# Gate and up projections by seven products: four of a pair's products summed in one PSUM bank and two in another, and taken in another order

## The chip, the cores and the metric

The kernel runs on one core of one Trainium2 chip. The metric is the device time of one execution in microseconds (us). A core has a TensorE (PE) that multiplies matrices, a VectorE (DVE), a ScalarE (ACT) and a GpSimd (POOL) for element-wise work, and DMA queues. TensorE writes its results to eight accumulation banks (PSUM), from which DVE and ACT read.

## The reference, cut to what matters

One decoder layer over 1056 tokens (1024 of a prompt, 32 of eight samples), all in float32: a mixing sub-layer, then a SwiGLU feed-forward, then a gated per-layer input. The change is in the feed-forward:

```python
f = _rms(x, n_ffn_pre)
f = (jax.nn.silu(f @ w_gate) * (f @ w_up)) @ w_down      # 1024 -> 2816 -> 1024
x = x + _rms(f, n_ffn_post)
x = x + jax.nn.sigmoid(x @ w_ple_gate) * (p @ w_ple)
```

## The kernel before, in words

The tokens stand in three groups of 352 (groups 0, 1, 2). Each float32 operand is split into a high and a low part (`split`, L162 to L165: an ACT cast makes the high part, a DVE subtraction the low part), and a product of a weight block and an operand is three matmuls of 128x352 per block of 128 rows: high by high, high by low, low by high.

The feed-forward has 22 columns of 128 hidden channels, two to a *slab*. A column (the code calls one call of `gate_up` a slot: slot 0 and slot 1 of a slab) has a gate weight `wg` and an up weight `wu`. For token group 2 a column is done directly: 24 matmuls for the gate, 24 for the up. Groups 0 and 1 together are done by a seven-product scheme (a 2x2 block product with seven multiplications instead of eight): seven products of 12 matmuls each. Two use a half of `wg` by itself (with the operands `B11` and `B21`), one a half of `wu` (operand `T4`), and four use sums of both weights (`S1` with `T1`, `S2` with `T2`, `S3` with `T3`, `S4` with `B22`). GpSimd makes the four sums, in place in the raw weights (`w_sums`, L980), after `wg` and `wu` have been split; then they are split themselves into two tiles, one with S2 and S4, one with S1 and S3 (in the trace, tiles `sh` and `sl`).

The list `WALK` sets the order: steps 0 to 4 do slabs 0 to 4 for group 2 alone, steps 5 to 10 do slabs 5 to 10 for all three groups (below: three-group steps), steps 11 to 15 do slabs 0 to 4 for groups 0 and 1 (below: two-group steps). Slot 0 of each step has, after its first products, the down projections of the step before (`pending`): 24 or 16 products of six matmuls.

What sets the order: TensorE's matmuls are pinned in program order (`mm`, L126). The other engines' instructions are put in order by a scheduler at build time and then run strictly in that order. Split weights live in a ring of eight buffers, tag `wp` (`w_tile`; a high and a low tile each, so four weights at a time), raw weights in a ring of three, tag `wr`. Weights are made in the order of the list `ITEMS`, up to four items ahead of the one in use (`need`). A new tile takes the buffer that comes free first in the program, and its writer waits until TensorE has read the old tile there for the last time. PSUM tiles (`bank`) come from a ring of eight in the same way.

In `gate_up` before the change, every product takes a bank of its own, and the sums of products are made on DVE: `p1` (first product, copied by ACT at L1019), then adds of a product each (`add`, L1014).

Of the kernel before, what the change touches and what calls it, by code (L numbers as in the profile page):

```python
# [13 lines left out]
ALU = mybir.AluOpType  # L14
# [47 lines left out]
def trunk_kernel(  # L62
# [61 lines left out]
    def mm(*args, **kw):  # L124

        ins = te.matmul(*args, **kw)  # L126
        if pinned[0]:
            tc.keep_in_program_order(ins)

    def bank():  # L130
        return psum.tile([P, 512], F32, tag="b", name=nm("b"))

    def tmp(n, s="t", dt=F32):
        return spool.tile([P, n], dt, tag="tmp", bufs=6, name=nm(s), padded_shape=[P, NX])
# [138 lines left out]
                    w_load(js[0])  # L273
        return made[k]

    def gemm(ps, ops, start=True, stop=True):

        last = len(ops) - 1
        for i, (wh, wl, xh, xl) in enumerate(ops):
            mm(ps, wh, xh, start=start and i == 0, stop=False)  # L280
            mm(ps, wh, xl, start=False, stop=False)
            mm(ps, wl, xh, start=False, stop=stop and i == last)

    def ops8(w, xs):

# [703 lines left out]
    def ops4(w, x):  # L989

        return [(w[0][:, k, :], w[1][:, k, :], x[0][:, k, :], x[1][:, k, :]) for k in range(4)]

    def quarter(w, h):
        return tuple(t[:, 4 * h : 4 * h + 4, :] for t in w)

    def gate_up(items, slot, gs, pending):

        ig, iu, is_ = items
        n = N

# [12 lines left out]
        def add(out, a, ps):  # L1013
            ve.tensor_tensor(out, a, ps, op=ALU.add)  # L1014

        wg = need(ig)
        if 0 in gs:
            p1 = tmp(n, "p1")
            se.copy(p1, product(quarter(wg, 0), f7["B11"]))  # L1019
        if 2 in gs:  # L1020
            sl = tmp(n, "sl")
            se.activation(sl, direct(wg), AF.Silu)
        if 0 in gs:
            c11 = tmp(n, "c11")
            add(c11, p1, product(quarter(wg, 1), f7["B21"]))
# [4 lines left out]
        if 2 in gs:  # L1030
            ve.tensor_tensor(sl, sl, direct(wu), op=ALU.mult)
        for g in gs:
            if slot == 0:
                new_hid[g] = half(g, F32R, "hid")
        if 2 in gs:
            hid_put(2, slot, sl)
        if pending and 0 not in gs:
            pending()
        if 0 not in gs:
            return  # L1040
# [7 lines left out]
        if 2 in gs:  # L1048
# [8 lines left out]
        se.activation(p1, p1, AF.Silu)  # L1057
        ve.tensor_tensor(u3, u3, p1, op=ALU.mult)
        hid_put(1, slot, u3)

    os_ = [None] * G

# [203 lines left out]
```

## Time and profile before

| | |
|---|---|
| time, median of 3 runs | 1122.58 us (1121.98 to 1122.92) |
| the profiled execution's own time | 1121.84 us |
| its span, first to last instruction | 1120.1 us |
| TensorE busy | 1108.9 us (99%) |
| DVE, ACT, POOL busy | 748.4, 440.7, 179.5 us |

The span is what the rows below are laid out on: times in them are us from its start. An engine's busy time counts its instructions; the time in which it waits stands as idle time before an instruction, with what ended it. Steps 5 to 10 run from about 388 to 790 us, steps 11 to 15 from there to about 980 us.

### The profile page before, as it was taken

How to read it: one execution, taken by the hardware profiler on the slowest of the kernel's cores; microseconds unless marked ns; L12 is line 12 of the kernel's file. 1: busy time of each engine (PE TensorE's matmuls, PEld its weight loads, DVE VectorE, ACT ScalarE, POOL GpSimd, SP SyncE). 2: the span in 40 equal slices, each digit the busy share in tenths (PEclk: the TensorE clock that was granted, in tenths of full speed). 3: DMA queues.
4: the chain of work that ended last, by engine and by line, in shares of the span. 5: the costliest groups of instructions: out<-in, count | busy, mean ns of one | idle time of the engine just before them, and what ended most of it. 6: DMA issues, size and time to landing. Idle time of an engine off the chain costs nothing.

```text
span 1120.1 us, 17702 instructions
## 1 busy us (share of the span) xinstructions
PE 1108.9 (99%) x7171; PEld 1090.8 (97%) x7171; DVE 748.4 (67%) x1244; ACT 440.7 (39%) x782; POOL 179.5 (16%) x152
## 2 busy tenths in 40 slices
PE   8999999999999999999999999999999999999998
PEld 8999988899999999999999999999999999999998
DVE  6667468985879955355554555557887877789532
ACT  8323276664646524331321314124424334366220
POOL 0045132200000041011111101111132123100000
PEclk9999999999999999999999999999999999999999
DMA  8121311272543312111110212112212222246211
GB/s 288 57 70 43 119 41 38 83 265 71 206 159 132 114 38 76 39 61 54 38 57 20 75 38 76 39 39 93 104 57 77 74 76 79 96 161 215 91 58 39
DMA packets 35265, 99.54 MB, mean 89 GB/s; under 512 B 4180, under 2 KB 14708, under 8 KB 35184
## 3 DMA queue, kind: packets, MB, share of 16 engines
q1 hardware_dynamic: 33856, 96.65, 25.6%
q10 hardware_dynamic: 1328, 1.77, 0.5%
q8 instruction: 56, 0.92, 0.4%
q14 instruction: 25, 0.20, 0.1%
HBM read 88.30 MB, written 10.11 MB: 88 GB/s over the span
## 4 chain that ended last, share of the span: by engine, by line
PE 88%; DVE 6%; ACT 3%; DMA 1%; issue 1%; POOL 0%; SPq 0%; DVEq 0%; ACTq 0%; POOLq 0%
PE b L126 88%; ACT a L634 1%; DVE wl L165 1%; DMA xr<-in_x_dram 1%; DVE mx L626 1%; DVE a L671 1%; ACT wh L164 1%; POOL wr L980 0%; DVE h L366 0%; PE b L120 0%; DMA c<-in_gains_dram 0%; DVE o L1107 0%; DVE x L1111 0%; DVE a L734 0%; DVE p L1014 0%
## 5 line engine op out<-in xcount | busy, mean ns | idle before, releaser
L126 PE MATMUL b<-fh,wh 128*128 128x352 f32 x808 | 260.7, 323 | 0.0
L126 PE MATMUL b<-fh,wl 128*128 128x352 f32 x808 | 259.3, 321 | 0.0
L126 PE MATMUL b<-fl,wh 128*128 128x352 f32 x808 | 259.0, 321 | 0.0
L126 PE MATMUL b<-hid,wh 128*128 128x352 f32 x1056 | 252.5, 322 | 1.7 <-DVE o L1107 1.2
L164 ACT CAST wh<-wr 128x1024 fp32r<-128x1024 f32 (+1 forms) x139 | 142.9, 1030 | 249.6 <-PE b L126 206.6
L165 DVE TENSOR_TENSOR wl<-wr,wh 128x1024 fp32r<-128x1024 f32 (+1 forms) x139 | 171.7, 1238 | 63.8 <-ACT wh L164 63.6
L126 PEld LDWEIGHTS b<-hid,wh 128*128 128x128 f32 x1056 | 182.3, 188 | 2.5 <-issue 1.5
L126 PE MATMUL b<-hid,wl 128*128 128x352 f32 x528 | 169.0, 320 | 0.0
L980 POOL TENSOR_TENSOR wr<-wr 128x512 f32<-128x512 f32 x44 | 63.4, 1441 | 622.3 <-DVE wl L165 451.8
L126 PEld LDWEIGHTS b<-fl,wh 128*128 128x128 f32 x808 | 151.8, 188 | 0.0
L126 PEld LDWEIGHTS b<-fh,wl 128*128 128x128 f32 x808 | 151.8, 188 | 0.0
L126 PEld LDWEIGHTS b<-fh,wh 128*128 128x128 f32 x808 | 151.6, 188 | 0.0
L1077 DVE TENSOR_TENSOR o<-o,b 128x352 f32<-128x352 f32 x240 | 114.7, 514 | 27.3 <-PE b L126 27.2
L126 PE MATMUL b<-fh,sh 128*128 128x352 f32 x352 | 113.6, 323 | 0.0
L126 PE MATMUL b<-fl,sh 128*128 128x352 f32 x352 | 112.8, 320 | 0.0
L126 PE MATMUL b<-fh,sl 128*128 128x352 f32 x352 | 112.7, 320 | 0.0
L126 PE MATMUL b<-h,wh 128*128 128x352 f32 x480 | 106.1, 327 | 1.3 <-ACT h L364 0.9
L165 DVE TENSOR_TENSOR sl<-wr,sh 128x1024 fp32r<-128x1024 f32 x44 | 53.7, 1222 | 75.5 <-ACT sh L164 75.5
L126 PEld LDWEIGHTS b<-hid,wl 128*128 128x128 f32 x528 | 99.0, 187 | 0.0
L164 ACT CAST sh<-wr 128x1024 fp32r<-128x1024 f32 x44 | 45.7, 1047 | 130.9 <-POOL wr L980 91.3
L126 PEld LDWEIGHTS b<-h,wh 128*128 128x128 f32 x480 | 82.6, 190 | 2.6 <-DVE h L366 1.3
L126 PE MATMUL b<-h,wl 128*128 128x352 f32 x240 | 66.3, 325 | 0.0
(150 smaller groups left out, 1593.3 us busy)
## 6 DMA issues: line engine op xcount, KB each, us to landing
wr<-in_w_gu_dram SPq DMA_DIRECT2D x64, 512.0 KB, 3.3
wr<-in_w_dn_dram SPq DMA_DIRECT2D x32, 512.0 KB, 3.5
wr<-in_w_pg_dram SPq DMA_DIRECT2D x14, 512.0 KB, 3.7
x<-in_x_dram SPq DMA_DIRECT2D x6, 704.0 KB, 7.7
x1d<-x SPq DMA_DIRECT2D x6, 704.0 KB, 3.5
x<-x1d SPq DMA_DIRECT2D x6, 704.0 KB, 6.2
out_y_dram<-yo SPq DMA_DIRECT2D x24, 176.0 KB, 1.8
wr<-in_w_out_b_dram SPq DMA_DIRECT2D x8, 512.0 KB, 3.3
```

What stands on the lines that cost most here:

```text
L126: ins = te.matmul(*args, **kw)
L164: fix(se.copy(hi, src))
L165: fix(ve.tensor_tensor(lo, src, hi.bitcast(F32), op=ALU.subtract))
L626: ve.tensor_reduce(mx, t, axis=AX.X, op=ALU.max)
L634: se.activation(t[:, c, :], t[:, c, :], AF.Exp, bias=nmx[:, c : c + 1], scale=scale, accum_out=sm[:, c : c + 1])
L671: ve.copy_predicated(tk, m4(0).bitcast(mybir.dt.int32), v4(cur[kv]))
L980: ge.tensor_tensor(out, a, b, op=op)
L1077: ve.tensor_tensor(o, o, v, op=ALU.add)
```

## The change

Products of one pair are no longer all in banks of their own. A bank `row` takes the first gate product (operand `B11`), is copied out as `p1`, and stays: later products are added onto it by TensorE (no start flag), and it is read again between them. A bank `col` takes the product S1 and, after that has been copied out, S4 on top. In a three-group step `row` takes four products (B11, S2, S3, T4) and is read after each; in a two-group step it takes three, and T4 has its own bank. DVE adds go from seven of a product each to three (three groups) or four (two groups); ACT gets two or three more copies of a bank (L1023 of the changed kernel). The order of the products changes: in a three-group step from gate, direct gate, gate, direct up, S2, S3, T4, S1, S4 to gate, direct gate, gate, S1, S2, S4, S3, direct up, T4; in a two-group step from gate, gate, T4, S2, S3, S1, S4 to gate, gate, S1, S2, T4, S3, S4.

```diff
-    def gemm(ps, ops, start=True, stop=True):
+    def gemm(ps, ops, start=True, stop=True, onto=False):
...
-            mm(ps, wh, xh, start=start and i == 0, stop=False)
...
+            mm(ps, wh, xh, start=start and i == 0, stop=False, skip_group_check=onto)
...
-        def product(w, x):
-            ps = bank()
-            gemm(ps[:, :n], ops4(w, x))
+        def product(w, x, ps=None, start=True):
+            onto = ps is not None
+            ps = ps if onto else bank()
+            gemm(ps[:, :n], ops4(w, x), start, onto=onto)
             turn(12)
             return ps[:, :n]
...
-        def add(out, a, ps):
+        def add(a, ps, s):
+            out = tmp(n, s)
             ve.tensor_tensor(out, a, ps, op=ALU.add)
+            return out
+
+        def copied(ps, s):
+            out = tmp(n, s)
+            se.copy(out, ps)
+            return out
...
         if 0 in gs:
-            p1 = tmp(n, "p1")
-            se.copy(p1, product(quarter(wg, 0), f7["B11"]))
+            row = bank()
+            p1 = copied(product(quarter(wg, 0), f7["B11"], row), "p1")
...
-        if 2 not in gs:
+        s = need(is_)
+        col = bank()
+        p5 = copied(product(s["S1"], f7["T1"], col), "p5")
+        u2 = copied(product(s["S2"], f7["T2"], row, False), "u2")
+
+        def c12():
+            t = add(u2, product(s["S4"], f7["B22"], col, False), "c12")
+            se.activation(t, t, AF.Silu)
+            return t
+
+        if third:
+            g1 = c12()
+            u1 = add(p5, product(s["S3"], f7["T3"], row, False), "u1")
+            ve.tensor_tensor(u1, u1, g1, op=ALU.mult)
+            hid_put(1, slot, u1)
+            third_up()
+            ve.tensor_tensor(c11, c11, product(quarter(wu, 1), f7["T4"], row, False), op=ALU.mult)
+            hid_put(0, slot, c11)
+        else:
             p4 = product(quarter(wu, 1), f7["T4"])
-        s = need(is_)
-        add(p1, p1, product(s["S2"], f7["T2"]))
-        u3 = tmp(n, "u3")
-        add(u3, p1, product(s["S3"], f7["T3"]))
-        c21 = tmp(n, "c21")
-        if 2 in gs:
-            p4 = product(quarter(wu, 1), f7["T4"])
-        add(c21, u3, p4)
-        ve.tensor_tensor(c21, c21, c11, op=ALU.mult)
-        hid_put(0, slot, c21)
-        p5 = product(s["S1"], f7["T1"])
-        add(u3, u3, p5)
-        add(p1, p1, p5)
-        add(p1, p1, product(s["S4"], f7["B22"]))
-        se.activation(p1, p1, AF.Silu)
-        ve.tensor_tensor(u3, u3, p1, op=ALU.mult)
-        hid_put(1, slot, u3)
+            ps = product(s["S3"], f7["T3"], row, False)
+            u3 = copied(ps, "u3")
+            u1 = add(p5, ps, "u1")
+            ve.tensor_tensor(u3, u3, p4, op=ALU.add)
+            ve.tensor_tensor(u3, u3, c11, op=ALU.mult)
+            hid_put(0, slot, u3)
+            g1 = c12()
+            ve.tensor_tensor(u1, u1, g1, op=ALU.mult)
+            hid_put(1, slot, u1)
```

**TensorE, step 14 (two groups), from slot 0's T4 on.** One row for the first of a product's 12 matmuls. The operands are `fh_4142` T4, `fh_4137` T2, `fh_4097` T3, `fh_3829` T1, `fh_4037` B22, `fh_3708` B11, `fh_3906` B21. Before:

```order
L126 MATMUL b_9115<-fh_4142,wh_8839 128x352
...
L126 MATMUL b_9134<-fh_4137,sh_8916 128x352
...
L126 MATMUL b_9149<-fh_4097,sh_8920 128x352
...
L126 MATMUL b_9168<-fh_3829,sh_8920 128x352
...
L126 MATMUL b_9183<-fh_4037,sh_8916 128x352
...
L126 MATMUL b_9208<-fh_3708,wh_8961 128x352
...
L126 MATMUL b_9223<-fh_3906,wh_8961 128x352
...
L126 MATMUL b_9242<-fh_4142,wh_9029 128x352
...
L126 MATMUL b_9261<-fh_4137,sh_9103 128x352
```

After:

```order
L126 MATMUL b_9102<-fh_4142,wh_8778 128x352
...
L126 MATMUL b_8878<-fh_4097,sh_8872 128x352
...
L126 MATMUL b_9073<-fh_4037,sh_8868 128x352
...
L126 MATMUL b_9159<-fh_3708,wh_8913 128x352
...
L126 MATMUL b_9174<-fh_3906,wh_8913 128x352
...
L126 MATMUL b_9200<-fh_3829,sh_9059 128x352
...
L126 MATMUL b_9159<-fh_4137,sh_9055 128x352
```

From the end of slot 0's T4 to slot 1's first product with a sum there were seven products, and there are four. That first product used the tile of S2 and S4 (`sh_9103`); now it uses the tile of S1 and S3 (`sh_9059`).

**ACT, the same place.** Here `wh_8981` is the high part of slot 1's `wu`, `sh_9055` and `sh_9059` are those of the sums (S2 with S4, S1 with S3), `wr_` are raw weights. After:

```order
L1023 COPY u_9100<-b_8878 128x352
L164 CAST wh_8981<-wr_8876 128x1024
L1023 COPY u_9127<-b_8878 128x352
L164 CAST hid_9065<-u_9127 128x352
L164 CAST sh_9055<-wr_8782 128x1024
L1060 ACTIVATE c_9147<-c_9147 128x352
L164 CAST sh_9059<-wr_8876 128x1024
```

In the built program the cast of `wh_8981` waits for the last high-part matmul of slot 0's T4, whose weight `wh_8778` stood in its buffer. Before, the cast of `wh_9029` (slot 1's `wu`) waited for slot 0's T4 too (weight `wh_8839`). In the three-group steps the buffer for slot 1's `wu` is now that of slot 0's S2 and S4, so that its cast waits for S4. The cast of S1 and S3 is still behind that of S2 and S4, now with a Silu (L1060) between.

**DVE, step 12, slot 0.** `hid_` is the low part of group 1's hidden block of the slot before, `sl_` the low part of S2 and S4, `c_` the gate sum. Before:

```order
L1107 TENSOR_TENSOR o_3284<-o_3284,b_8017 128x1408
L1058 TENSOR_TENSOR u_8024<-u_8024,p_7950 128x352
L1111 SCALAR_TENSOR_TENSOR x_7871<-o_3284,c_72,x_7871 128x352 x2
L165 TENSOR_TENSOR hid_7829<-u_8024,hid_7829 128x352
L1014 TENSOR_TENSOR c_8106<-p_8091,b_8107 128x352
L165 TENSOR_TENSOR sl_8082<-wr_7704,sh_8081 128x1024
```

After:

```order
L1129 TENSOR_TENSOR o_3284<-o_3284,b_7970 128x1408
L165 TENSOR_TENSOR hid_7780<-u_8003,hid_7780 128x352
L1133 SCALAR_TENSOR_TENSOR x_7824<-o_3284,c_72,x_7824 128x352 x2
L1080 TENSOR_TENSOR u_8005<-u_8005,c_8023 128x352
L165 TENSOR_TENSOR sl_8034<-wr_7656,sh_8033 128x1024
L165 TENSOR_TENSOR hid_7781<-u_8005,hid_7781 128x352
L1018 TENSOR_TENSOR c_8073<-p_8056,b_8058 128x352
```

The hidden block's low part and the gate sum stood ahead of `sl_` and now stand behind it.

More of the change, by code (lines that the diff above doesn't have):

```diff
@@ L274, in need @@
         return made[k]
-    def gemm(ps, ops, start=True, stop=True):
+    def gemm(ps, ops, start=True, stop=True, onto=False):
         last = len(ops) - 1
         for i, (wh, wl, xh, xl) in enumerate(ops):
-            mm(ps, wh, xh, start=start and i == 0, stop=False)
-            mm(ps, wh, xl, start=False, stop=False)
-            mm(ps, wl, xh, start=False, stop=stop and i == last)
+            mm(ps, wh, xh, start=start and i == 0, stop=False, skip_group_check=onto)
+            mm(ps, wh, xl, start=False, stop=False, skip_group_check=onto)
+            mm(ps, wl, xh, start=False, stop=stop and i == last, skip_group_check=onto)
     def ops8(w, xs):
@@ L1011, in direct @@
             return ps[:, :n]
-        def add(out, a, ps):
+        def add(a, ps, s):
+            out = tmp(n, s)
             ve.tensor_tensor(out, a, ps, op=ALU.add)
+            return out
[3 more added lines that the diff above has]
+            return out
+        third = 2 in gs
         wg = need(ig)
         if 0 in gs:
-            p1 = tmp(n, "p1")
-            se.copy(p1, product(quarter(wg, 0), f7["B11"]))
-        if 2 in gs:
+            row = bank()
+            p1 = copied(product(quarter(wg, 0), f7["B11"], row), "p1")
+        if third:
             sl = tmp(n, "sl")
@@ L1023, in gate_up @@
         if 0 in gs:
-            c11 = tmp(n, "c11")
-            add(c11, p1, product(quarter(wg, 1), f7["B21"]))
+            c11 = add(p1, product(quarter(wg, 1), f7["B21"]), "c11")
             se.activation(c11, c11, AF.Silu)
@@ L1029, in gate_up @@
         wu = need(iu)
-        if 2 in gs:
-            ve.tensor_tensor(sl, sl, direct(wu), op=ALU.mult)
         for g in gs:
```

10 lines of the change are left out of this document (6 added, 4 removed).

## The prediction, made before the changed kernel was timed

> **What bounds the kernel now.** I read the page first: its first line, the busy times and the chain that ended last.
>
> ```profile
> span 1120.1 us, 17702 instructions
> PE 1108.9 (99%) x7171; PEld 1090.8 (97%) x7171; DVE 748.4 (67%) x1244; ACT 440.7 (39%) x782; POOL 179.5 (16%) x152
> PE 88%; DVE 6%; ACT 3%; DMA 1%; issue 1%; POOL 0%; SPq 0%; DVEq 0%; ACTq 0%; POOLq 0%
> ```
>
> TensorE works 99% of the span, and the chain lies on it. Next the table by stage, over the feed-forward, with TensorE's waits in its last part (windows, then waits from 800 to 1000 us):
>
> ```profile
> core 0: us, PE busy (x) PEld busy (x) DVE busy (x) ACT busy (x) POOL busy (x), PEclk, DMA share, GB/s
> 400.00:800.00 400.00, 400.00 (x2523) 400.00 (x2522) 226.76 (x376) 115.99 (x178) 69.59 (x52) 1.00 0.17 55
> 800.00:900.00 100.00, 98.29 (x615) 97.57 (x614) 83.17 (x126) 38.27 (x53) 22.37 (x16) 1.00 0.25 80
> 900.00:1000.00 100.00, 100.00 (x635) 100.00 (x634) 75.47 (x125) 40.87 (x59) 22.14 (x16) 1.00 0.28 90
> PE b L126 <- DVE o L1107: 1.2, 1, 1.2
> PE b L126 <- DVE hid L165: 0.5, 1, 0.5
> ```
>
> From 400 to 800 us TensorE has no gap at all; from 800 to 1000 it loses 1.7 us, at two waits for DVE. So relieving DVE can win 2 us at most, and the changed kernel issues the same matmuls. The question is only whether the new order makes TensorE wait.
>
> **The change: what it removes and adds.** The rows for the two kinds of work (groups by line, DVE and ACT):
>
> ```profile
> L1014 DVE TENSOR_TENSOR p<-p,b 128x352 f32<-128x352 f32 x66 | 34.0, 515 | 6.1 <-PE b L126 5.5
> L1019 ACT COPY p<-b 128x352 f32<-128x352 f32 x22 | 9.7, 442 | 0.9 <-PE b L126 0.9
> ```
>
> DVE loses four adds in each of the 12 three-group pairs and three in each of the 10 two-group pairs: 78 x 0.515 = 40 us. ACT gains two and three copies: 54 x 0.442 = 24 us. Both lie under a TensorE that is 100% busy, with DVE at 57% from 400 to 800 us and ACT at 29%: I cost them at nothing. Were the cover gone, they would be worth what TensorE waits for these engines, the 1.7 us above.
>
> **The wait that it moves: the split sums.** In slot 1 of a two-group step the sums S1 to S4 can be made only after slot 1's `wu` has been split, and its cast waits for the buffer that slot 0's T4 product reads. Step 14 shows the whole chain (timeline, four engines; `wh` is the cast of `wu`, `sh` the casts of the sums, `sl` their low parts):
>
> ```profile
> 918.96 0.32 PE L126 MATMUL b<-fh,wl 128*128 128x352 f32 x1
> 919.12 0.32 PE L126 MATMUL b<-fh,sh 128*128 128x352 f32 x1
> 932.46 0.32 PE L126 MATMUL b<-fh,sh 128*128 128x352 f32 x1
> 919.20 1.05 ACT L164 CAST wh<-wr 128x1024 fp32r<-128x1024 f32 x1 [0.85 <-PE b L126]
> 920.28 1.23 DVE L165 TENSOR_TENSOR wl<-wr,wh 128x1024 fp32r<-128x1024 f32 x1 [0.68 <-ACT wh L164]
> 921.64 1.29 POOL L980 TENSOR_TENSOR wr<-wr 128x512 f32<-128x512 f32 x1 [13.56 <-DVE wl L165]
> 923.02 2.90 POOL L980 TENSOR_TENSOR wr<-wr,wr 128x512 f32<-128x512 f32 x2
> 926.00 1.45 POOL L980 TENSOR_TENSOR wr<-wr 128x512 f32<-128x512 f32 x1
> 927.48 2.00 ACT L164 CAST sh<-wr 128x1024 fp32r<-128x1024 f32 x2 [2.20 <-POOL wr L980]
> 928.57 1.23 DVE L165 TENSOR_TENSOR sl<-wr,sh 128x1024 fp32r<-128x1024 f32 x1 [1.83 <-ACT sh L164]
> 930.14 1.22 DVE L165 TENSOR_TENSOR sl<-wr,sh 128x1024 fp32r<-128x1024 f32 x1
> 930.26 0.50 ACT L1057 ACTIVATE p<-p 128x352 f32<-128x352 f32 x1 [0.78 <-DVE p L1014]
> ```
>
> Slot 0's T4 is done at 919.12 (call it 0). The sums leave POOL at 927.45 (8.33), their casts end at 929.48 (10.36), their low parts at 929.80 and 931.36 (10.68 and 12.24). TensorE meanwhile does seven products, 13.34 us or 1.906 each, and takes up S2, whose tile came first, at 932.46: 2.7 us in hand, without a gap.
>
> Now only four products lie between (S3, S4, and slot 1's B11 and B21): 4 x 1.906 = 7.62 us. And the first sum wanted is S1, whose tile comes second. Its first two matmuls need the cast alone, the third (0.32 us on) the low part: 7.94. I put the chain together in the changed queues. Up to POOL's end, 8.33, it is unchanged. ACT casts S2 and S4 to 9.4, then the Silu (0.50) that now stands between, then S1 and S3 to about 10.9. DVE makes the first low part to 10.7, then a multiplication (about 0.5) that waits for this Silu, to 11.1, then the second low part (1.22), to 12.3. TensorE goes on at 12.35 instead of 7.94: **4.4 us lost in slot 1 of each two-group step, 5 x 4.4 = 22.0 us**. Queued behind the waiting matmul on TensorE is everything else, so the loss is paid in full. In step 11 part of it falls earlier: there the copy of S2 out of `row` stands behind the cast of `wu` on ACT, so S3 waits some 2 us, and S1 that much less. Bounds: 3.9 if the Silu costs nothing, 4.9 if POOL is as slow as in step 12 and the rest slips with it; 19.5 to 24.5 us.
>
> Slot 0 of these steps has 16 down products before its sums and is not late. In the three-group steps the chain of slot 1 takes (timeline of one, from slot 0's T4 on):
>
> ```profile
> 606.58 0.32 PE L126 MATMUL b<-fh,sh 128*128 128x352 f32 x1
> 618.51 0.52 DVE L165 TENSOR_TENSOR hid<-u,hid 128x352 fp32r<-128x352 f32 x1
> ```
>
> 12.0 us to the end of the last `sl`, just ahead of the second row. Now it starts at the end of slot 0's S4, and S1 comes after S3, T4, B11, B21 and two direct products as long as two each: 8 x 1.906 = 15.2 us. In the changed queues the cast of S1 and S3 stands behind a cast of `hid`, which waits for DVE, which is held at the first low part until about 10.7; that adds 2 us, to some 14.1. It is in time by 1.4 us: nothing, with 6 x 1 us as the upper end.
>
> **The reads between products.** TensorE must not add to a bank before it has been read. S4 follows the copy of S1 with one product between, 1.906 us; a copy is 0.44 and starts about 0.2 after the product. 1.2 us are left, enough for one cast of 1.05 ahead of it on ACT. In the built order none stands there but in step 11 (counted above). I take nothing.
>
> **DVE in step 12, slot 0.** The second wait above, in rows:
>
> ```profile
> 819.97 0.33 PE L126 MATMUL b<-hid,wh 128*128 128x352 f32 x1
> 820.80 0.43 PE L126 MATMUL b<-hid,wh 128*128 128x352 f32 x1 [0.51 <-DVE hid L165]
> 819.13 1.61 DVE L165 TENSOR_TENSOR hid<-u,hid 128x352 fp32r<-128x352 f32 x1
> 821.47 1.22 DVE L165 TENSOR_TENSOR sl<-wr,sh 128x1024 fp32r<-128x1024 f32 x1 [0.30 <-ACT sh L164]
> ```
>
> The down product at 819.97 waits for `hid`, 0.67 us beyond its cadence. In the changed order `hid` stands behind `sl`, which ends at 822.69, so `hid` comes at about 823.2, where it came at 820.74: **+2.5 us** (0 to +3.5). The other wait, 1.2 us for the bank that L1107 reads, in step 13, should shrink, since DVE has fewer adds ahead: **-1.2** (-2.0 to 0; `row` now holds one of the eight banks there, against it).
>
> **The clock.** What a gap of 4 us does to it, from windows at the start, in the middle and at the end:
>
> ```profile
> 4.95:8.37 3.42, 2.15 (x8) 1.25 (x8) 2.70 (x6) 2.92 (x6) 0.00 (x0) 1.00 1.02 341
> 8.37:11.79 3.42, 3.42 (x13) 3.42 (x13) 2.36 (x5) 2.10 (x5) 0.00 (x0) 0.50 1.02 357
> 865.11:868.52 3.41, 2.20 (x15) 1.94 (x13) 2.91 (x3) 1.52 (x2) 0.00 (x0) 1.00 0.16 41
> 868.52:871.93 3.41, 3.41 (x22) 3.41 (x23) 3.41 (x8) 0.00 (x0) 0.00 (x0) 1.00 0.29 113
> 1114.29:1117.70 3.41, 1.36 (x9) 1.07 (x7) 1.04 (x2) 0.46 (x1) 0.00 (x0) 1.00 0.00 0
> 1117.70:1120.10 2.40, 0.00 (x0) 0.00 (x0) 0.00 (x0) 0.00 (x0) 0.00 (x0) 0.50 0.20 75
> ```
>
> The granted clock changes at multiples of 3.41 us. After a stretch with 8 matmuls, and after one with 1.36 us busy, it was 0.50 in the next; after one with 15 it stayed 1.00. A gap of 4.4 us leaves one stretch with at least 2.2 us idle, wherever it falls, so I expect a half-clock stretch behind each. A full one does 13 matmuls instead of 22: 9 x 0.159 = 1.4 us; partly under the gap, 1.3. Four gaps of slot 1 and that of step 12 make **5 x 1.3 = 6.5 us** (0 to 10, the latter with two stretches for some).
>
> The Trainium skill has a rule on this, "TensorE: Matmul & The Clock Gate", section "HAM oscillation — how this bites in real kernels": in short, no idle gaps over about 3.4 us. By the table in the same page's "What's actually happening" the clock drops after a whole idle window; here S1's first two matmuls break the gap, and it would stay. The last rows above speak against so strict a reading.
>
> **Sum.** 22.0 + 2.5 - 1.2 + 6.5 = 29.8 us on 1121.84, the profiled execution's own time (its span and 1.7 us around it): 1151.6. The median of the runs is 0.7 above that execution: **1152 us**.
>
> **Rivals.**
> - *The clock stays at 1.00*, if two matmuls in the gap or a partly busy stretch are enough. For it: the stretch with 15 matmuls. Against it: the one with 1.36 us busy. 1121.84 + 22.0 + 2.5 - 1.2 + 0.7 = 1146.
> - *The three-group steps wait too*: their margin of 1.4 us is eaten by ACT, where the `hid` cast ahead of the sums waits for a DVE that is itself late. Six slots of 1 us, and clock with some: 1152 + 9 = 1161. Against it: ACT is 29% busy there.
> - *Not slower: the sums are in time and DVE's relief is what remains.* Slot 1's chain would have to be shorter than 7.94 us. For it: 78 fewer instructions ahead on DVE, and the two waits of 1.7 us gone give 1121. Against it: cast, low part and POOL alone end at 8.33, and none of these waited for DVE's adds in the rows above.
>
> **How the numbers follow.** The forecast 0.68, clock stays 0.16, three-group waits 0.08, not slower 0.08. The likeliest's own range is 1146 to 1159. With the low ends (19.5 + 0 - 2.0 + 0 = 17.5 on 1122.5) and the high ones (24.5 + 3.5 + 10 = 38) it is 1140 to 1161, which takes in the second case and most of the third. A measurement of this kernel can tell about 0.2% from no change. Of the last case half would be over 0.2% faster, half within it: faster 0.04, same 0.04, slower 0.92.
>
> **What would show it.** Between about 790 and 1000 us TensorE's row should lose some 25 us in five gaps, each before the third matmul of an S1 product (`b<-fh,sl`), ended by DVE's `sl`; one of 3 us before a `hid` matmul in step 12; and clock of 0.50 after them. From 400 to 800 us it should have no gap. DVE's busy time should fall by 40 us and ACT's rise by 24. No gap before S1, or one ended by something else than the sums, would prove the chain wrong; a gap of the right size with the clock at 1.00, the second case.

## The result

The changed kernel takes **1162.49 us** (median of 5 runs, 1161.75 to 1166.45) where the kernel before takes 1122.29 us (median of 5 runs, 1121.98 to 1122.92) beside it: a ratio of 1.0365 with a 95% interval of 1.0353 to 1.0376, **40 us slower**. The forecast was 1152 us with a range of 1140 to 1161. The direction, the place and the main mechanism were right. The size was 10 us short, and the measured time lies above the range: the terms for `hid` and for the clock were too small.

### The profile page after: what moved, and what is told of

The parts are those of the page before. It is cut to its first block, busy times and chain, and to the rows that moved or that the text cites. A ratio compares the mean times of both kernels' runs of the same rounds, so it can differ in the third digit from the quotient of the medians.

```text
span 1160.3 us, 17669 instructions
## 1 busy us (share of the span) xinstructions
PE 1124.6 (97%) x7171; PEld 1100.8 (95%) x7171; DVE 722.0 (62%) x1166; ACT 465.1 (40%) x836; POOL 180.9 (16%) x152
## 4 chain that ended last, share of the span: by engine, by line
PE 78%; DVE 7%; ACT 5%; POOL 4%; DMA 3%; issue 1%; SPq 0%; POOLq 0%; ACTq 0%; DVEq 0%
PE b L126 78%; POOL wr L981 4%; DVE wl L165 2%; DMA wr<-in_w_gu_dram 1%; ACT wh L164 1%; DVE sl L165 1%; ACT a L635 1%; DMA xr<-in_x_dram 1%; ACT sh L164 1%; DVE mx L627 1%; DMA a<-in_dmask_dram 1%; DMA x<-x1d 1%; DVE a L672 1%; SPq L341 0%; DVE h L367 0%
## 5 line engine op out<-in xcount | busy, mean ns | idle before, releaser
L126 PE MATMUL b<-hid,wh 128*128 128x352 f32 x1056 | 255.2, 324 | 6.5 <-DVE hid L165 3.7
L126 PE MATMUL b<-fh,sh 128*128 128x352 f32 x352 | 117.8, 335 | 14.0 <-ACT sh L164 12.3
L126 PE MATMUL b<-fh,sl 128*128 128x352 f32 x352 | 117.3, 333 | 5.0 <-DVE sl L165 5.0
L126 PE MATMUL b<-fl,sh 128*128 128x352 f32 x352 | 116.3, 330 | 0.0
L126 PEld LDWEIGHTS b<-fh,sh 128*128 128x128 f32 x352 | 69.1, 196 | 15.7 <-ACT sh L164 13.7
```

## The profile after

First the page of the changed kernel (its first line, the busy times, the shares of the chain that ended last):

```profile
span 1160.3 us, 17669 instructions
PE 1124.6 (97%) x7171; PEld 1100.8 (95%) x7171; DVE 722.0 (62%) x1166; ACT 465.1 (40%) x836; POOL 180.9 (16%) x152
PE 78%; DVE 7%; ACT 5%; POOL 4%; DMA 3%; issue 1%; SPq 0%; POOLq 0%; ACTq 0%; DVEq 0%
```

The matmuls are the same 7171; the span has grown by 40.2 us, and TensorE has 78% of the chain where it had 88%. POOL, which had 0%, has 4%: the chain now runs through GpSimd's sums. Then the same windows as before the change, and TensorE's waits from 800 to 1000 us (us in total, times, longest):

```profile
400.00:800.00 400.00, 397.51 (x2504) 396.93 (x2503) 208.58 (x322) 127.50 (x202) 66.19 (x49) 1.00 0.17 55
800.00:900.00 100.00, 89.08 (x525) 86.52 (x524) 65.38 (x94) 36.24 (x54) 21.01 (x15) 0.97 0.20 64
900.00:1000.00 100.00, 91.76 (x541) 89.84 (x541) 58.86 (x86) 36.21 (x55) 22.44 (x17) 0.95 0.19 64
PE b L126 <- ACT sh L164: 9.4, 4, 2.9
PE b L126 <- DVE hid L165: 3.7, 5, 1.6
PE b L126 <- DVE sl L165: 3.3, 4, 0.9
PE b L126 <- ACT hid L164: 1.7, 1, 1.7
PE b L126 <- DVE o L1099: 1.1, 1, 1.1
```

From 800 to 1000 us TensorE does 1066 matmuls where it did 1250. It waits for the split sums (`sh`, `sl`) and for `hid`, and the clock is below 1.00. The chain behind the wait for the sums, in step 13, from slot 0's T4 to slot 1's S1 (timeline of the changed kernel, four engines):

```profile
899.02 0.32 PE L126 MATMUL b<-fh,wl 128*128 128x352 f32 x1
899.23 1.05 ACT L164 CAST wh<-wr 128x1024 fp32r<-128x1024 f32 x1 [1.24 <-PE b L126]
900.30 1.23 DVE L165 TENSOR_TENSOR wl<-wr,wh 128x1024 fp32r<-128x1024 f32 x1 [4.45 <-ACT wh L164]
901.66 1.29 POOL L981 TENSOR_TENSOR wr<-wr 128x512 f32<-128x512 f32 x1 [18.80 <-DVE wl L165]
906.11 1.28 POOL L981 TENSOR_TENSOR wr<-wr 128x512 f32<-128x512 f32 x1
907.42 1.04 ACT L164 CAST sh<-wr 128x1024 fp32r<-128x1024 f32 x1 [3.56 <-POOL wr L981]
908.37 0.49 ACT L1060 ACTIVATE c<-c 128x352 f32<-128x352 f32 x1
908.77 1.03 ACT L164 CAST sh<-wr 128x1024 fp32r<-128x1024 f32 x1
910.07 1.22 DVE L165 TENSOR_TENSOR sl<-wr,sh 128x1024 fp32r<-128x1024 f32 x1
906.65 0.32 PE L126 MATMUL b<-fh,wl 128*128 128x352 f32 x1
909.85 0.66 PE L126 MATMUL b<-fh,sh 128*128 128x352 f32 x1 [2.87 <-ACT sh L164]
911.35 0.66 PE L126 MATMUL b<-fh,sl 128*128 128x352 f32 x1 [0.54 <-DVE sl L165]
```

T4 ends at about 899.2. POOL is done at 907.39 (8.2 after it; the forecast had 8.33), the second cast at 909.80 (10.6; 10.9), the second low part at 911.29 (12.1; 12.3). TensorE was done with its four products at 906.81 and stands until 909.85, then again for the low part.

To size the rest I took all matmul starts after 225 us. Back to back they are 158.9 ns apart; what an interval has beyond that is put down by what stands behind it: a matmul of one of the sums, a matmul of `hid`, any other, an interval of about 293 ns in a stretch at half clock, or a spacing a little above 158.9 ns.

| beyond 158.9 ns, us | before | after | difference |
|---|---|---|---|
| waits before products of sums (S1 to S4) | 0.1 | 21.9 | +21.8 |
| waits before products of `hid` | 2.6 | 8.6 | +5.9 |
| half clock | 0.0 | 10.4 | +10.4 |
| other waits | 2.1 | 3.1 | +1.0 |
| spacing | 1.6 | 2.0 | +0.4 |
| sum | 6.4 | 45.8 | +39.5 |

The spans differ by 40.2, so 0.7 us lie ahead of 225 us or behind the last matmul.

## The experiments

Each kernel below is the changed kernel with the edit shown, unless it says otherwise. Ratios are to runs of the kernel before on the same chip (medians 1122.1 to 1123.6 us). The table gives the same accounting for each profiled execution; the span less what its row lists (and less the added work in two of them) lies between 1113.5 and 1115.5 us in all, so no large cost is left out of it. "Hid ahead" means that the split of slot 0's first sums is kept behind `hid`.

| kernel | median us | span | before sums | before `hid` | half clock | other | spacing |
|---|---|---|---|---|---|---|---|
| changed | 1162.5 | 1160.3 | 21.9 | 8.6 | 10.4 | 3.1 | 2.0 |
| old banks, new order | 1153.3 | 1151.8 | 18.5 | 3.8 | 10.0 | 2.8 | 2.2 |
| T4 first | 1148.5 | 1145.7 | 9.7 | 13.8 | 3.0 | 3.0 | 2.0 |
| S3 and S1 split first | 1137.8 | 1137.3 | 9.3 | 5.8 | 1.6 | 3.5 | 2.6 |
| gap filled (20.7 us added) | 1155.9 | 1152.3 | 3.6 | 9.3 | 0.0 | 2.9 | 1.8 |
| fresh bank for S2, S3 | 1174.8 | 1174.9 | 26.2 | 7.5 | 15.2 | 5.4 | 6.4 |
| T4 first, S3 last | 1154.6 | 1154.0 | 1.1 | 20.0 | 7.1 | 3.0 | 8.6 |
| S1, T4, S2, S4, S3 | 1156.2 | 1152.8 | 3.0 | 23.4 | 6.7 | 2.1 | 3.7 |
| T4 first, hid ahead | 1141.1 | 1136.9 | 9.7 | 5.9 | 2.2 | 3.1 | 2.5 |
| T4, S2, S1, S3, S4, hid ahead | 1133.8 | 1132.6 | 3.6 | 7.3 | 2.7 | 2.1 | 3.2 |
| the same, group 2 later | 1136.1 | 1135.7 | 6.3 | 3.3 | 1.5 | 2.2 | 8.6 |
| changed, hid ahead, group 2 later | 1162.8 | 1156.1 | 20.3 | 5.9 | 11.5 | 2.4 | 2.4 |
| two-group half alone | 1160.6 | 1157.8 | 21.4 | 8.3 | 10.6 | 2.1 | 1.9 |
| three-group half alone | 1129.8 | 1129.3 | 1.1 | 2.6 | 0.0 | 3.1 | 7.0 |
| the same, wait filled (1.3 us added) | 1124.6 | 1122.8 | 0.1 | 2.6 | 0.0 | 3.0 | 1.5 |

### Order or banks?

The first two kernels take the change apart: one keeps the new order and takes the shared banks away, the other keeps the shared banks and puts T4 back to the front. In the kernel **before**, with the new order of the two-group steps:

```diff
-        if 2 not in gs:
-            p4 = product(quarter(wu, 1), f7["T4"])
         s = need(is_)
+        if 2 not in gs:
+            p5 = product(s["S1"], f7["T1"])
         add(p1, p1, product(s["S2"], f7["T2"]))
+        if 2 not in gs:
+            p4 = product(quarter(wu, 1), f7["T4"])
```

> The kernel before, with every product in a bank of its own and all adds on DVE; only the order of the products in the two-group steps is that of the change (gate, gate, S1, S2, T4, S3, S4). Theory (order): gaps before S1 in slot 1 of steps 11 to 15, 4 us each, and half clock behind them: 20 + 6 to 10 us, and something for DVE, which is busier here: 1149 to 1165 us. Rival (shared banks): no more than 1125 us.

1153.33 us, ratio 1.0263 (1.0247 to 1.0278). Nearly three quarters of the loss come with the order alone, 18.5 us of it before the sums and 10.0 in half clock. The rival falls. The other side:

```diff
+        if not third:
+            p4 = product(quarter(wu, 1), f7["T4"])
         s = need(is_)
         col = bank()
...
         else:
-            p4 = product(quarter(wu, 1), f7["T4"])
             ps = product(s["S3"], f7["T3"], row, False)
```

> The changed kernel, but in the two-group steps the T4 product stands ahead of S1 again, as before the change; the shared banks and everything else stay as changed. Theory (the order of the products makes the loss: T4 of slot 0 now ends only four products ahead of S1 of slot 1): seven products, 13.3 us, lie between again, the chain of 12.3 us is in time, the gaps before S1 in slot 1 and the half-clock stretches behind them go, some 20 + 8 us; what stays is the waits in slot 0 of steps 12 to 15 and the ends, 0 to 8 us: 1122 to 1131 us, 1127 as a single number. Rival (the shared banks make the loss: a bank must be read before TensorE may add to it): nothing changes but the place of the gaps, 1150 us or more.

1148.47 us, ratio 1.0225 (1.021 to 1.024): between the two. The gaps before S1 are gone, as the theory says, and 7 us of half clock with them, but two other waits stand there (TensorE's waits, 790 to 1000 us):

```profile
PE b L126 <- DVE hid L165: 6.2, 4, 3.6
PE b L126 <- ACT u L1023: 5.3, 9, 0.6
PE b L126 <- ACT hid L164: 5.1, 4, 1.6
```

The second row is the price of the shared bank: with T4 moved away S3 follows S2 into the same bank, and TensorE waits for ACT's copy each time, 0.6 us as this view has it and 0.70 to 0.76 us beyond the spacing of the matmuls. In the changed order T4 stood between and hid it. The waits for `hid` are taken up below.

### The chain of the sums

GpSimd makes the sums S1 and S3 first. Splitting their tile first shortens the chain to S1 and leaves the order of the matmuls alone:

```diff
-        for src in (a1, a2):
+        for src in (a2, a1):
...
-        (s24, s31) = two
+        (s31, s24) = two
```

> The changed kernel, but of the two tiles of sums the one that holds S3 and S1 is split first; the order of the products stays. GpSimd makes these two sums first, so the split can start two sums (2.7 us) earlier and is one cast and one low part (2.3 us) shorter for S1. Theory (TensorE waits for the end of this chain): S1 is ready at about 7.6 us after T4 of slot 0, wanted at 7.9, so its gap goes; S2, wanted 1.9 us later, comes at 10.6 and waits 0.8 to 1.5 us; five small gaps, no half clock behind them: 1125 to 1138 us, 1131 as a single number. Rival (what is late is the freeing of a buffer or a bank in the end, not the split): the order of two tiles changes nothing, 1158 us or more.

1137.83 us, ratio 1.0129 (1.0107 to 1.0151): two edited lines give back 24.7 of the 40 us, half clock included. This is the strongest evidence for the chain. The expectation had S2 wait 0.8 to 1.5 us for its own tile. S2 does wait about 1.0 us each time, but for something else:

```profile
PE b L126 <- ACT p L1023: 5.1, 5, 1.1
```

S2 waits not for its own low part but for the copy of the bank `row` that it adds to (`p`, the first gate product): the copy stands in ACT's queue behind the cast of the other sums, which waits for GpSimd. A shared bank makes TensorE wait for whatever is queued ahead of its reader.

### What the half clock costs

```diff
         col = bank()
+        if not third and slot == 1:
+            for _ in range(26):
+                th = f7["T1"][0]
+                mm(col[:, :n], th[:, 0, :P], th[:, 0, :], start=True, stop=True)
```

> The changed kernel with 26 matmuls added that nobody reads (128x352, 0.159 us each, 4.1 us in all) ahead of S1 in slot 1 of the two-group steps, so that TensorE works where it now waits. Theory (four of the gaps are followed by stretches of 3.41 us at half clock, six of the seven in all, and each costs some 1.4 us): the clock stays at 1.00 there, and though 5 x 4.1 us of work are added the time falls by 6 to 10 us, to some 1154 us. Rival (the half clock is under waits that are there anyway): no change, 1161 to 1164 us.

1155.88 us, ratio 1.029 (1.0273 to 1.0307): 6.6 us faster by the medians than the changed kernel, with 20.7 us of useless matmuls added, and no stretch at half clock left in the feed-forward. The half clock is a cost of its own, some 7 to 10 us here.

### The waits before hid

The third term, hid in slot 0, was the one most wrong. Step 12 of the changed kernel (timeline, ACT and DVE; the first `hid` cast and low part are group 0's, the second group 1's):

```profile
819.80 1.05 ACT L164 CAST wh<-wr 128x1024 fp32r<-128x1024 f32 x1 [2.40 <-DMA wr<-in_w_gu_dram]
820.75 0.48 ACT L164 CAST hid<-u 128x352 fp32r<-128x352 f32 x1
828.30 1.04 ACT L164 CAST sh<-wr 128x1024 fp32r<-128x1024 f32 x1 [6.33 <-POOL wr L981]
829.25 0.48 ACT L164 CAST hid<-u 128x352 fp32r<-128x352 f32 x1
822.02 1.61 DVE L1129 TENSOR_TENSOR o<-o,b 128x1408 f32<-128x1408 f32 x1
823.55 0.52 DVE L165 TENSOR_TENSOR hid<-u,hid 128x352 fp32r<-128x352 f32 x1
823.99 3.14 DVE L1133 SCALAR_TENSOR_TENSOR x<-o,c,x 128x352 f32<-128x352 f32 x2
829.38 1.23 DVE L165 TENSOR_TENSOR sl<-wr,sh 128x1024 fp32r<-128x1024 f32 x1 [0.72 <-ACT sh L164]
830.52 0.52 DVE L165 TENSOR_TENSOR hid<-u,hid 128x352 fp32r<-128x352 f32 x1
```

Each `hid` stands behind something that waits: group 0's cast behind a cast that waits for its weights' transfer, its low part behind the end of the group 2 work (`o`), group 1's cast behind the cast of the sums, which waits for GpSimd, and its low part behind `sl`. To see whether this queueing is the cause, the split of slot 0's first sums is kept behind what was issued before it. In the kernel with T4 first this moves one cast and one low part behind `hid` in steps 12 to 15, and nothing else:

```diff
+            fixed[0] = pin_sums[0]
             split(*hl, src)
+            fixed[0] = False
...
+        pin_sums[0] = slot == 0 and not third and pending is not None
         wg = need(ig)
+        pin_sums[0] = False
```

> The kernel with T4 first in the two-group steps (1148.5 us), with one edit: in slot 0 of these steps the split of the first tile of sums is kept behind what stands ahead of it in the program. In the queues that moves one cast on ACT and one low part on DVE behind the cast and the low part of group 1's hid, in steps 12 to 15, and nothing else. Theory (the waits for hid in slot 0 are queueing: the cast of hid, ready at 871.8 us in step 13, stands behind a cast of sums that waits for GpSimd until 874.35, and TensorE waits 3.2 us there): these waits of about 3 us in each of steps 12 to 15 go, 9 to 13 us with their clock: 1133 to 1141 us, 1137 as a single number; the ten waits for the copy of S2 stay. Rival (hid is late because its last product, S4 or S3, ends late): 1146 us or more.

1141.05 us, ratio 1.0162 (1.014 to 1.0184), against 1148.47 without the edit: 7.4 us by the medians, 8.8 by the spans, a little less than expected because step 12's wait stayed; the waits before `hid` fall from 13.8 to 5.9 us. Steps 13 to 15 have none left for `hid` itself, only one of 1.1 us for a bank. Queueing it is, in these three steps.

The same with the products of the two-group steps in an order in which no two that share a bank are neighbours (the three-group steps keep theirs):

```diff
-        p5 = copied(product(s["S1"], f7["T1"], col), "p5")
-        u2 = copied(product(s["S2"], f7["T2"], row, False), "u2")
+        if third:
+            p5 = copied(product(s["S1"], f7["T1"], col), "p5")
+            u2 = copied(product(s["S2"], f7["T2"], row, False), "u2")
+        else:
+            u2 = copied(product(s["S2"], f7["T2"], row, False), "u2")
+            p5 = copied(product(s["S1"], f7["T1"], col), "p5")
```

> As the run before it, and the products of the two-group steps in the order gate, gate, T4, S2, S1, S3, S4, so that a product stands between any two that share a bank. Theory (all of the loss is these three things: the chain of the sums from T4's end, a bank read between adjacent products, and the queue ahead of hid): no wait over 1.5 us is left between 790 and 1000 us, and the time is 1121 to 1130 us, 1126 as a single number. Rival (with these gone another step of the chain is late in its place): 1134 us or more.

1133.79 us, ratio 1.0098 (1.0082 to 1.0114). It lies above the theory's range and a hair below the rival's. With three things undone, 29 of the 40 us are back; waits of up to 1.0 us remain at several places, and one of 4 us in step 12, before group 0's `hid`, with 2.7 us of half clock behind it. Its rows (DVE):

```profile
817.89 3.10 DVE L1144 SCALAR_TENSOR_TENSOR x<-o,c,x 128x352 f32<-128x352 f32 x2
820.91 1.58 DVE L165 TENSOR_TENSOR hid<-u,hid 128x352 fp32r<-128x352 f32 x1
```

So I gave the last work on group 2 to DVE later, in this kernel and in the changed one:

```diff
-            chain(ple_steps(2), 19)
+            chain(ple_steps(2), 59)
```

> The order T4, S2, S1, S3, S4 with the split of the sums kept behind hid (1133.8 us), and one edit: the last work on token group 2 (the adds of the final residual, made while step 12 runs) is given to DVE later, so that it stands behind hid in step 12. In the run before, hid's low part of group 0 waited there behind two such operations (3.1 us), TensorE lost 4.8 us in slot 0 of step 12 and ran two stretches at half clock behind it. Theory (that wait is DVE's queue): 4 to 7 us less, 1125 to 1130 us, 1128 as a single number. Rival (GpSimd, which works on the sums at the same time and during which these operations take 1.5 us each, slows hid wherever it stands): 1132 us or more.

1136.14 us, ratio 1.0112 (1.0092 to 1.0132): not faster, the rival's time but not its mechanism. The wait of 4 us in step 12 did go, one of 1.2 us before group 1's `hid` came in its place, and the waits before `hid` fell from 7.3 to 3.3 us; but in step 11 a new one of 2.6 us came before S2, for the copy of `row`: the moved work put other casts ahead of that copy on ACT. The rest of the difference is the spacing, 8.6 instead of 3.2 us (below).

> The changed kernel in its own order with both of these edits: in slot 0 of the two-group steps the split of the first tile of sums is kept behind hid, and the final work on group 2 comes later. Theory (the forecast's step on hid in step 12 was the right mechanism, and these two queues are what TensorE waited for there: 4.8 us): the waits of group 1's hid in step 12, 1.9 + 1.1 us, go, and with them half-clock stretch behind them; the gaps before S1 stay: 1155 to 1160 us, 1158 as a single number. Rival (the waits are there for another reason): 1161 to 1165 us.

1162.76 us, ratio 1.037 (1.0351 to 1.0389), in runs from 1157.9 to 1166.6: by the median nothing, so the expectation failed. The profiled execution, 1157.9, has 2.7 us less before `hid`. In step 12 group 0's wait of 1.8 us is gone, and so is the wait for group 1's cast; in place of group 1's two waits, 3.0 us, stands one of 2.4 us for its low part, because work on group 2 is still ahead of that on DVE (the first `hid` is group 0's, the second group 1's):

```profile
821.31 0.52 DVE L165 TENSOR_TENSOR hid<-u,hid 128x352 fp32r<-128x352 f32 x1
824.66 3.12 DVE L1139 SCALAR_TENSOR_TENSOR x<-o,c,x 128x352 f32<-128x352 f32 x2
827.69 0.52 DVE L165 TENSOR_TENSOR hid<-u,hid 128x352 fp32r<-128x352 f32 x1
```

A new wait of 0.5 us for a bank follows, and there are eight half-clock stretches instead of seven. The queue is what TensorE waited for in step 12, but the edit is worth less than the runs scatter, and the time of this term in the changed kernel stays an account from its trace.

Two orders put S3, whose end completes group 0's `hid`, last. One has T4 ahead of S1 as well; the other has T4 behind S1 and splits the tile of S3 and S1 first. The edit that both share:

```diff
+            g1 = c12()
             ps = product(s["S3"], f7["T3"], row, False)
...
-            g1 = c12()
```

> The changed kernel with another order in the two-group steps: gate, gate, T4, S1, S2, S4, S3. T4 comes first as before the change, and S4 stands between S2 and S3, so that the copy of S2 out of its bank has a product's time before S3 is added there. With T4 first but S2 and S3 side by side TensorE waited for this copy in each of the ten slots, 0.6 us more than its cadence. Theory (the chain of the sums and the reads between adjacent products account for the loss, the rest are waits for the low part of hid in slot 0): ten waits go, 7 us with their share of clock, and the time is 1122 to 1143 us, 1135 as a single number. Rival (two banks read between products are dear wherever the products stand): no change from 1148 us.

> The changed kernel with two edits in its two-group steps: the tile with the sums S3 and S1 is split first, and the order is gate, gate, S1, T4, S2, S4, S3. From T4 of slot 0 to S1 of slot 1 lie five products, 9.5 us, and S1's chain is 7.6 us; S2 is wanted 3.8 us after S1, and ready at 10.6. Theory: no gap before S1 or S2 in slot 1, the waits for hid in slot 0 remain: 1122 to 1140 us, 1132 as a single number. Rival (S1 is late for another reason than the length of the chain from T4): 1145 us or more.

1154.62 us, ratio 1.027 (1.0257 to 1.0283), and 1156.16 us, ratio 1.0288 (1.0273 to 1.0303). Both expectations of the time failed. The waits before the sums went as expected (1.1 and 3.0 us are left), and those before `hid` grew to 20.0 and 23.4. By the order of the program, S3 last lets both groups' last multiplications and splits start only then, and the next step's down products come two products (3.8 us) later. The order before the change had S3 third of five, which left more time; that this is the whole reason is not shown.

### Is it the bank held over slot 0?

```diff
         s = need(is_)
+        if not third:
+            row = bank()
...
-        u2 = copied(product(s["S2"], f7["T2"], row, False), "u2")
+        ps2 = product(s["S2"], f7["T2"], row, not third)
+        u2 = copied(ps2, "u2") if third else add(p1, ps2, "u2")
...
-            u3 = copied(ps, "u3")
-            u1 = add(p5, ps, "u1")
+            u3 = add(p1, ps, "u3")
+            u1 = tmp(n, "u1")
+            ve.tensor_tensor(u1, p5, u3, op=ALU.add)
```

> The changed kernel, but in the two-group steps the first gate product's bank is given back after its copy, and S2 and S3 take a fresh bank; DVE adds the copy again. The order stays. Theory (in slot 0 of these steps the bank held over 16 down products makes TensorE wait for the next bank, 3 us in steps 13 to 15): these waits go or fall to 1.5 us as in the kernel before, the gaps before S1 stay at 4 us each: 1156 to 1161 us. Rival (these waits are DVE's order and not the number of banks): the waits stay at 3 us, 1161 to 1165 us.

1174.8 us, ratio 1.0442 (1.042 to 1.0463): slower, as neither said. The waits in slot 0 of steps 13 to 15 are 2.4 us instead of 3.0. The one among them that was for a bank, 1.2 us in step 13, is gone, so the held bank is at most a part of them; the kernel before, with no bank held there, had that wait too. But S2's bank is now read by DVE, and TensorE waits for that read:

```profile
825.88 0.43 PE L126 MATMUL b<-fh,sh 128*128 128x352 f32 x1 [4.24 <-DVE u L1018]
```

### The halves, and a spacing that lasts

The two halves of the change alone; first the two-group half:

> The other half of the change: the three-group steps as before it, the two-group steps as changed. Theory (the two-group steps account for all but a wait of 0.9 us and its effect on the spacing): 1157 to 1164 us, 1161 as a single number. Rival (the halves act on each other, through what the three-group steps leave in the queues): below 1155 us.

1160.62 us, ratio 1.0334 (1.0316 to 1.0352). The two-group steps are the loss. This is 7 us more than the new order with the old banks by the medians, 8 by the ratios; the table has 2.9 us more before the sums and 4.5 us more before `hid`. That is what the shared banks, with the copies and queues that come with them, add in these steps. The three-group half alone:

> Half of the change: the three-group steps as changed (four products in one bank, two in another, new order), the two-group steps as before the change. Theory (the loss arises in the two-group steps; the three-group ones gave one wait of 1.1 us at their first slot and nothing else): 1121 to 1125 us, 1123 as a single number, and TensorE with no more than 1.5 us of gaps from 400 to 790 us. Rival (the new three-group steps leave DVE's and ACT's queues so that what follows is late, and are part of the 10 us by which the whole change costs more than its order alone): 1127 us or more.

1129.76 us, ratio 1.0039 (1.0024 to 1.0054), in runs from 1124.1 to 1131.1: the rival's size, but not its mechanism. TensorE has the one wait of 0.8 us for `sl` from 300 to 800 us and no other. The windows of this kernel, of the changed one, and of the kernel before show where the time is:

```profile
410.00:780.00 370.00, 370.00 (x2298) 370.00 (x2297) 182.27 (x271) 114.65 (x181) 64.78 (x48) 1.00 0.15 49
```

```profile
410.00:780.00 370.00, 370.00 (x2331) 370.00 (x2330) 188.79 (x286) 116.68 (x184) 64.75 (x48) 1.00 0.15 51
```

```profile
410.00:780.00 370.00, 370.00 (x2331) 370.00 (x2330) 201.40 (x334) 105.14 (x162) 64.12 (x48) 1.00 0.16 51
```

TensorE is busy without a gap in all three, at a clock of 1.00, and does 33 matmuls fewer in the first: their starts are 161.1 ns apart instead of 158.9. The changed kernel has the same three-group steps and, in its profiled execution, 158.9. So the spacing is not the code's. In the first kernel it changes at the wait at 404 us. With that wait filled:

```diff
+        if pending and begun and len(begun) == 8:
+            for _ in range(8):
+                th = f7["T1"][0]
+                mm(col[:, :n], th[:, 0, :P], th[:, 0, :], start=True, stop=True)
```

> The kernel with only the three-group half of the change (1129.8 us median of runs from 1124.1 to 1131.1), with 8 matmuls added that nobody reads (0.159 us each, 1.3 us) ahead of S1 in slot 0 of step 5, where TensorE waited 0.9 us for the low part of the sums. In its profile the spacing of the matmuls was 161.1 ns from there to 790 us, where the kernel before and the changed kernel have 158.9. Theory (a wait can set another spacing, which then lasts until the next wait, here 2400 matmuls and 5.3 us): without the wait the spacing is 158.9 as before the change, and the runs lie within 1.5 us of each other at 1123 to 1126 us. Rival (the spacing does not come from the wait): spread and median as without the edit, plus 0.4 us.

1124.58 us, ratio 1.0014 (1.0004 to 1.0024): 5.2 us faster by the medians, 2.8 by the ratios, with 1.3 us of work added; the runs still spread over 3.4 us, not 1.5. A second execution of the kernel without the filling:

> The kernel with only the three-group half once more, unchanged. Its first profile had 161.1 ns between matmuls from 406 to 790 us in an execution of 1131.1 us; its other runs went down to 1124.1. Theory (the spacing, set anew by the wait at 404 us, makes the difference): an execution below 1127 us shows 158.9 ns there, one above 1128 us shows 161.1. Rival (spacing and time are not tied): a pairing the other way.

1128.67 us, with 161.1 ns there. That fits, but no execution below 1127 us of this kernel was profiled. Over all profiled executions: of the eleven with the wait at 404 us six have 158.9 ns from 410 to 780 us and five 161.1; the six without it (the kernel before, the filled one, and four others here) all have 158.9. That the wait brings the wider spacing about in some executions is likely by this count, but not shown.

No version here beats the kernel before, and none was to be expected to by much: its feed-forward waits 1.7 us in all.

## Why the prediction came out 10 us short

**The bound, and what DVE's relief is worth: right.** TensorE was the limit, and 26 us less on DVE (40 forecast) bought nothing: the three-group half alone, with 48 of the 78 adds gone, is no faster either. ACT rose by 24.4 us, as forecast. DVE fell by less mainly because more of its multiplications and `hid` subtractions fall beside GpSimd's sums and take up to three times as long (next section but one): what they take beyond 0.52 us each adds up to 14 us now and 4 before.

**The split sums in slot 1: right.** 22.0 us were forecast in five gaps; in the two-group steps 20.9 were measured (21.9 less the three-group wait), 3.9 to 4.3 a step, and in step 11 the first 1.9 of them fall before S3, at the copy of S2, as the prediction had it. The gaps end at the rows it named. Undoing the order, or shortening the chain, removes them.

**`hid` in slot 0: the step that failed.** "+2.5 (0 to +3.5)" for step 12 and "-1.2" for the bank in step 13 make +1.3; measured were +4.1 and +1.8, +5.9 together. What was priced at 2.5 came: the low part of group 1's `hid` does stand behind `sl`, and group 1 waits 3.0 us where it waited 0.7. But the prediction saw one of four queues. Group 0's `hid` waits 1.8 us as well, behind a cast that waits for a transfer and behind the work on group 2. Group 0's low part is late in steps 13 to 15 too, by 0.3, 0.3 and 1.1 us. And the credit of 1.2 us, for fewer adds on DVE, did not come: the bank wait of step 13 went from 1.2 to 1.1 us. What `hid` waits for are casts and low parts that wait for GpSimd and for transfers, and fewer adds do not bring these forward.

**The clock: the mechanism right, the term too small.** 6.5 us were forecast for five stretches of 1.3 us, with an upper end of 10; seven stretches cost 10.4, 1.5 each. The prediction counted five gaps, those of slot 1 in steps 12 to 15 and the one before `hid` in step 12, with one stretch each. These five it was (the gap of step 11 fell in two parts and had none), but those in steps 13 and 15 have two stretches: the second half of the gap falls into the half-clock stretch and leaves too few matmuls in it as well. The rival "the clock stays", 1146 us, is refuted.

**The three-group steps: nearly right.** One wait of 1.05 us in the first slot instead of none, inside the bound of 6 us. That a wider spacing can begin there and last for the next 385 us, 5.3 us in some executions, was not thought of; it explains part of the spread of the changed kernel's runs at best, and its profiled execution has none of it.

**The reads between products: right, for the reason given.** Nothing was forecast but step 11, because a product stands between each copy and the next product into its bank. With T4 moved away from between S2 and S3, TensorE paid 0.70 to 0.76 us at each such read; and a product between is not enough where the copy is held up in ACT's queue, as with S3 and S1 split first.

**The sum.** -1.1 (sums) + 4.6 (`hid`) + 3.9 (clock) + 1.05 (three groups) + 1.4 (other waits and spacing) is 9.9 us on the 29.8 forecast: 39.7 of the 40.2 us by which the span grew. The range's upper end had +3.5 for `hid`, +24.5 for the sums and +10 for the clock: the sums came in below their end, and clock and `hid` above theirs.

## What to carry to other kernels

Where TensorE is full, taking work off another engine is worth nothing. An order of products is worth the slack that it leaves on each chain behind it: count the products between the last read of a buffer and the first use of what is made in it, for every buffer. Before an accumulator is shared and read between products, ask what stands in the reader's queue ahead of the copy, since TensorE then waits for that too. And cost a gap with its clock: here a gap of 4 us, where it was not split in two as in step 11, cost another 1.5 to 3 us.

## What the runs showed of the hardware

**The clock goes by the matmuls in a stretch.** Five stretches of 3.41 us around the gap of step 13 (windows of the changed kernel; behind the length stand the busy times and instructions of PE, PEld, DVE, ACT and POOL, then the granted clock, the third value from the end):

```profile
902.73:906.14 3.41, 3.41 (x23) 3.41 (x22) 1.99 (x4) 0.49 (x1) 3.17 (x4) 1.00 0.00 0
906.14:909.56 3.42, 0.84 (x6) 0.55 (x4) 1.06 (x1) 2.14 (x3) 1.25 (x1) 1.00 0.00 0
909.56:912.97 3.41, 2.58 (x7) 2.13 (x8) 3.41 (x6) 3.37 (x6) 0.00 (x0) 0.50 0.56 174
912.97:916.38 3.41, 3.41 (x13) 3.41 (x13) 1.86 (x2) 0.77 (x2) 0.00 (x0) 0.50 0.38 133
916.38:919.80 3.42, 3.42 (x24) 3.42 (x23) 0.00 (x0) 1.05 (x2) 0.00 (x0) 1.00 0.00 0
```

The stretch with 6 matmuls is followed by half clock, and the half-clock stretch with 7, though TensorE was busy 2.58 us of it, by another. Over the changed kernel and the eleven others that have half clock there, between 760 and 1045 us: of the stretches at full clock all 43 with at most 8 matmul starts were followed by half clock, and none of the 114 with 9 to 19. Of those at half clock all 15 with at most 8 were followed by another; with 9 one of two, with 10 to 12 none of 42. The Trainium skill, "TensorE: Matmul & The Clock Gate", section "What's actually happening", has the clock drop after at least one idle window; the trace does not agree, since a stretch with up to 8 matmuls, 1.3 us of work, is enough.

**A spacing that changes at a wait and lasts.** Matmuls of 128x352 start 158.9 or 161.1 ns apart on average, in the same code, without a gap and at a clock of 1.00; it changes at a wait and then holds for hundreds of microseconds (x2331 and x2298 in the rows above). What sets it was not found.

**DVE waits while GpSimd works, by the operands' place.** The same multiplication of the changed kernel in slot 1 of step 13 and in slot 0 of step 14, and GpSimd's sum beside the second:

```profile
909.64 0.52 DVE L1080 TENSOR_TENSOR u<-u,c 128x352 f32<-128x352 f32 x1
927.61 1.61 DVE L1080 TENSOR_TENSOR u<-u,c 128x352 f32<-128x352 f32 x1
927.39 1.45 POOL L981 TENSOR_TENSOR wr<-wr 128x512 f32<-128x512 f32 x1 [20.00 <-DVE wl L165]
```

It ends 0.4 us after GpSimd's instruction. Of its ten executions the four that fall on GpSimd's sums take 1.60 us, the other six 0.52. Adds that read one operand from a bank take 0.51 us on either side. The Trainium skill, "SBUF — State Buffer", section "SBUF: two separate sides", says that a DVE operation with two operands in SBUF and a GpSimd operation exclude each other for a whole instruction; the trace agrees. Low parts of `hid` that are made beside the sums take longer too: 13 of 32 such subtractions in the changed kernel took 0.76 to 0.99 us instead of 0.52, and the one in the step 12 rows of the order T4, S2, S1, S3, S4 took 1.58.
